# Attention's values in three chunks instead of four, their halves copied by ScalarE and added by GpSimd, one maximum for both context units

## The chip, the cores and the metric

The kernel runs on one core of a Trainium2 chip. The time is the device time of that core in microseconds; the profile is of one execution, taken by the hardware profiler. The engines are TensorE (PE, with its weight loads as PEld), VectorE (DVE), ScalarE (ACT), GpSimd (POOL) and SyncE (SP), which here only starts transfers. They run side by side and each works through its own queue in order.

## The reference

Two layers of a trunk over 1024 latent tokens (8 tiles of 128) and 256 context tokens (2 tiles), width 1024. In each layer a combined projection feeds a convolution, a retention and a latent attention; their outputs are joined, projected and normalised, and a gated feed-forward layer follows. The change touches the attention. It has 8 heads, queries and keys of 96 (64 without position, 32 with), values of 64:

```python
s = jnp.einsum('bqhd,bkhd->bhqk', qi, k).astype(jnp.float32) * scale
p = jax.nn.softmax(s, axis=-1).astype(v.dtype)
return jnp.einsum('bhqk,bkhd->bqhd', p, v)
...
attL = block_attention(qmL, jnp.concatenate([kmC, kmL], axis=1), jnp.concatenate([vmC, vmL], axis=1))
...
attC = block_attention(qmC, kmC, vmC)
```

Latent queries see all 1280 keys; context queries see the 256 context keys, and only in the first of the two layers.

## The kernel before, in words

**Units, batches, heads.** A unit is 128 queries of one head against all keys. Four units are a batch (512 queries), two batches a head, so a layer has 16 batches and 64 units. In layer 0 each head also has two context units (128 queries against 256 keys). One step of the loop at the end of the printed code handles one unit, and the order of the instructions on each engine is the order in which the code is run through (`manual_schedule`).

**A step.** `scores` multiplies queries and keys into a bank S (two such banks; each product is three matmuls, since both operands are split into a high and a low part) and VectorE takes the negative maximum nm. ScalarE writes P = exp(S + nm) and the sums. A step later VectorE transposes P in blocks of 32 x 32 into T (`block_transpose`). When the fourth unit of a batch is transposed, which is in step 0 of the next batch, `blocks` gathers the blocks of T into PT, twelve of sixteen by transfers that SyncE starts and four by GpSimd's copies.

**The values.** `weigh_chunk` multiplies PT with the values vr into a single bank po, in four chunks of 2, 2, 2 and 4 key tiles (`CHUNKS`); even key tiles add up in partitions 0 to 63 of po, odd ones in 64 to 127. The chunks of a batch run one per step from step 1 of the batch after next; the fourth thus falls on step 0 of the one after that. With the last chunk, TensorE spreads the reciprocal sums over a bank mm (L1011; mm is a single buffer too). `normalise` then copies and adds the two halves of po, multiplies by mm's copy on GpSimd and has `store` write the result.

**Context units.** `context_units` runs after the fourth unit of a head's second batch (of the first one in the last head). Both units' scores go into one mm bank, each followed by its own maximum. `direct_transposes` and `direct_weigh` follow one and two steps later and use mm as well.

**Deferred work.** Three lists hold it: `mids` is served between the scores and the exponential of a step, `soon` after the exponential, `steps` at the end of a step; the first argument of `later` is the number of steps. So loads of the next head (`load_head`, `load_v`; tiles kq and vr), the split of its keys and queries into high and low parts (`split_k`, `split_q`: kh and qh by ScalarE, kl and ql by GpSimd) and the stores all have a place by a number. SyncE's queue takes the loads, the gather of PT and the stores in the order in which they are issued.

Of the kernel before, what the change touches and what calls it, by code (L numbers as in the profile page):

```python
# [11 lines left out]
F32 = mybir.dt.float32  # L12
# [4 lines left out]
AX = mybir.AxisListType  # L17
# [26 lines left out]
def body(tc, I, out):  # L44
    nc = tc.nc
    mult, add, sub = ALU.mult, ALU.add, ALU.subtract

    def pool(name, bufs=1, space=None, side=None):
        kw = {}
        if space is not None:  # L50
            kw["space"] = space
        if side is not None:
            kw["side"] = side
        return tc.tile_pool(name=name, bufs=bufs, reuse_waits="tile", **kw)
# [6 lines left out]
    smp = es.enter_context(pool("small", 4))  # L61
# [14 lines left out]
    def bank(tag="mm", cols=512):  # L76
        return pools[tag].tile([128, cols], F32, name=tag, tag=tag)

    def tt(out, a, b, op, eng=None):
        (eng or nc.vector).tensor_tensor(out=out, in0=a, in1=b, op=op)  # L80
# [22 lines left out]
    def mms(ps, xs, start=True, stop=True):  # L103
        for i, (a, b) in enumerate(xs):
            nc.tensor.matmul(ps, lhsT=a, rhs=b, start=start and i == 0, stop=stop and i == len(xs) - 1)  # L105
# [404 lines left out]
    for l in range(L):  # L510
        last = l == L - 1
# [467 lines left out]
        pp_ = ats.enter_context(pool(f"attp{l}", 2, side="right"))  # L979
        tp_ = ats.enter_context(pool(f"attt{l}", 2, side="right"))  # L980
        sm_ = ats.enter_context(pool(f"atts{l}", 1, side="right"))
        CHUNKS = [range(0, 2), range(2, 4), range(4, 6), range(6, 10)]
        E0, E1, E2 = 6, 8, 8

        def scores(u, ps):

            nk = len(u.kts) * 128
            k0 = u.kts[0] * 128
            for c in range(0, nk, 512):
                n = min(512, nk - c)  # L990
                kc = slice(k0 + c, k0 + c + n)
                mms(ps[:, c:c + n], [(u.qh, u.hd.kh[:, kc]), (u.ql, u.hd.kh[:, kc]), (u.qh, u.hd.kl[:, kc])])
            u.nm = smp.tile([128, 1], F32, name="nm", tag="nm")
            nc.vector.reduce_max(out=u.nm, in_=ps[:, :nk], axis=AX.X, negate=True)  # L994
            u.ps = ps[:, :nk]

        def exponentials(u, P):

            nc.scalar.activation(out=P, in_=u.ps, func=AF.Exp, bias=u.nm, accum_out=u.sm)  # L999
            u.P = P  # L1000
# [16 lines left out]
        def blocks(us, T1):  # L1017
            PT = tp_.tile([128, 4, 4, 320], F32, name="PT", tag="PT")
            for s in range(4):
                for a in range(4):  # L1020
                    c = (a + s) % 4
                    o, i = PT[32 * c:32 * c + 32, a], T1[32 * a:32 * a + 32, c]
                    if s:
                        nc.sync.dma_start(out=o, in_=i)
                    else:
                        nc.gpsimd.tensor_copy(o, i)  # L1026
            us[0].PT = PT

        def weigh_chunk(us, i):
# [5 lines left out]
            src = u.PT.rearrange("p a u n -> p (a u) n")  # L1035
            for j in CHUNKS[i]:
                nc.tensor.matmul(u.po[64 * (j % 2):64 * (j % 2) + 64], lhsT=u.hd.v[:, j, :], rhs=src[:, :, j * 32:j * 32 + 32],  # L1037
                                 start=j < 2, stop=j > 7)
            if i < len(CHUNKS) - 1:
                return  # L1040
# [4 lines left out]
        def normalise(us, pr):  # L1045
            u = us[0]
            o = rawp.tile([128, 1024], F32, name="raw", tag="raw")
            o1, o2 = o[:64, :512], o[:64, 512:]
            nc.scalar.copy(o2, u.po[64:128])
            for i in range(2):  # L1050
                nc.scalar.copy(o1[:, 256 * i:256 * i + 256], pr[64 * i:64 * i + 64, :256])
            tt(o2, u.po[0:64], o2, add)
            tt(o1.rearrange("p (u a i) -> p u a i", u=4, a=4), o2.rearrange("p (a u i) -> p u a i", u=4, a=4),
               o1.rearrange("p (u a i) -> p u a i", u=4, a=4), mult, nc.gpsimd)
            steps.later(1, store, u.h, u.g, 0, o1)
# [32 lines left out]
        steps, mids, soon = Ticks(), Ticks(), []  # L1088
# [5 lines left out]
        def after(u, us, T1):  # L1094
# [6 lines left out]
            blocks(us, T1)  # L1101
            for i in range(len(CHUNKS)):
                mids.later(5 + i, weigh_chunk, us, i)
# [7 lines left out]
        def context_units(h):  # L1111
            us = []
            rc = rawp.tile([128, 1024], F32, name="raw", tag="raw")
            ps = bank("mm")
            sums = smp.tile([128, 4], F32, name="sums", tag="sums", bufs=6)
            for a in range(2):
                u = Unit()
                u.h, u.g, u.a, u.hd, u.kts, u.ending = h, 2, a * 128, heads[h], CTX, False
                u.qh, u.ql = (x[:, a * 128:a * 128 + 128] for x in qs[h, 2])
                u.sums, u.sm, u.t = sums, sums[:, a:a + 1], rc[:, 512:]  # L1120
                us.append(u)
                scores(u, ps[:, a * 256:])
            for a, u in enumerate(us):
                exponentials(u, rc[:, a * 256:a * 256 + 256])
            mids.later(2, direct_transposes, us)
            mids.later(3, direct_weigh, us)

        prev = None
        with tc.manual_schedule():
            for ti, (h, g) in enumerate(todo):  # L1130
                if ti == len(todo) - 1:
                    steps.later(E0, load_wo, 0, (0, 1))
                    steps.later(E1, split_wo, 0, (0, 1))
                    steps.later(E2, load_mixed, 0, 0)
                    steps.later(E2, load_mixed, 0, 1)
                    steps.later(E2, load_wo, 0, (2, 3))
                if g == 0:
                    if not last:
                        steps.later(1, split_q, h, 2)
                    if h:  # L1140
                        mids.later(1 if last else 2, load_v, h)
                    else:
                        steps.later(1, split_q, 0, 1)
                    if h < H_MLA - 1:
                        mids.later(1 if last else 2, load_head, h + 1)
                        steps.later(4, split_k, h + 1)
                        steps.later(5, split_q, h + 1, 0)
                        steps.later(7, split_q, h + 1, 1)
                us = []
                direct = ti == len(todo) - 1  # L1150
                T1 = tp_.tile([128, 4, 4, 320], F32, name="T1", tag="T1")
                sums = smp.tile([128, 4], F32, name="sums", tag="sums", bufs=6)
                for a in range(4):
                    u = Unit()
                    u.h, u.g, u.a, u.hd, u.kts, u.ending = h, g, a * 128, heads[h], kvt, ti == len(todo) - 1
                    u.qh, u.ql = (x[:, a * 128:a * 128 + 128] for x in qs[h, g])
                    u.sums, u.sm = sums, sums[:, a:a + 1]
                    us.append(u)
                    if direct:
                        P = T1.rearrange("p c u n -> p (c u n)")[:, a * NTOK:a * NTOK + NTOK]  # L1160
                    else:
                        P = pp_.tile([128, NTOK], F32, name="P", tag="P")
                    scores(u, bank("S", 1536))
                    mids.tick()
                    exponentials(u, P)
                    if prev is not None:
                        after(*prev)
                    late()
                    prev = (u, us, None if direct else T1)
                    if direct:  # L1170
                        u.t = pp_.tile([128, NTOK], F32, name="P", tag="P")
                        mids.later(1 + a, direct_transposes, [u])
                        mids.later(3 + a, direct_weigh, [u])
                    if not last and a == 3 and g == (h < H_MLA - 1):
                        context_units(h)
                    steps.tick()
            while mids.q or steps.q or soon:
                mids.tick()
                late()
                steps.tick()  # L1180
            split_wo(0, (2, 3))
# [60 lines left out]
        for i, t in enumerate(order):  # L1242
            ps = [firsts.pop(t) if i < 2 else project_out(t, 0), project_out(t, 1)]
# [8 lines left out]
            u = (rawp if late else w2).tile([128, 1024], F32, name="raw" if late else "u", tag="raw" if late else "u")  # L1252
# [104 lines left out]
        steps = {}  # L1357
# [33 lines left out]
        for j in range(NJ):  # L1391
            v = steps.pop(j) if j in steps else first_two(j)
            w, x, u, th1 = v.w, feat.op, v.u, v.th
# [133 lines left out]
        while ahead:  # L1527
# [26 lines left out]
            for t in range(4):  # L1554
                ps = bank("po")
# [34 lines left out]
        for t in tiles:  # L1590
# [4 lines left out]
            ps = [bank("mm") for _ in range(2)]  # L1595
# [123 lines left out]
```

## Time and profile before

| | |
|---|---|
| time, median of 3 runs | 3212.92 us (3206.94 to 3214.75) |
| profiled execution, own time | 3220.49 us |
| its span, first to last instruction | 3218.7 us |
| PE busy | 2974.4 us (92%) |
| DVE busy | 2308.2 us (72%) |
| POOL busy | 1490.9 us (46%) |
| ACT busy | 1194.7 us (37%) |
| mean granted TensorE clock | 0.953 |

The attention of layer 0 runs from about 449 to 745 us of the span, that of layer 1 from about 2170 to 2409. The shares of the whole span are averages over stages that are unlike each other, so the prediction reads these two by themselves. A granted clock of 1.00 is 2.4 GHz, 0.50 is 1.2 GHz. Times in a timeline are in us from the start of the span; a bracket at the end of a line is the engine's idle time ahead of it and what ended it.

### The profile page before, as it was taken

The page shows a single profiled execution, that of the slowest core. Times are in us where ns is not written, and L with a number is a line of the kernel's source. Part 1 is how long each engine was busy: PE and PEld are TensorE (multiplying, and loading weights), DVE is VectorE, ACT ScalarE, POOL GpSimd, SP SyncE. Part 2 cuts the span into 40 slices and gives each one's busy share as a digit, 9 for nine tenths or more (in the row PEclk, how much of TensorE's full clock was granted, in tenths as well). Part 3 has the DMA queues.
Part 4 walks back from the last instruction along what each step waited for, and adds up shares of the span by engine and source line. Part 5 has one row for each costly group of instructions (what it writes and reads, how often), then busy time and mean ns, then how long its engine had stood idle before and what let it go on. Part 6 is the DMA issues. An engine that isn't in the chain of part 4 may idle for free. (4 is left out here: it accounts for less than half of the span.)

```text
span 3218.7 us, 39711 instructions
## 1 busy us (share of the span) xinstructions
PE 2974.4 (92%) x13968; PEld 2303.3 (72%) x13968; DVE 2308.2 (72%) x3254; ACT 1194.7 (37%) x2354; POOL 1490.9 (46%) x1187
## 2 busy tenths in 40 slices
PE   7989998889979999999998898989999899999997
PEld 3677875556768888887786676776568678887685
DVE  4387556665887776654888868458966986666998
ACT  4223544444332222224332522445554322223432
POOL 2274535444332333324876355435654433333993
PEclk9999988889989999999999998998999999999998
DMA  7421156656622222223212521146865232223313
GB/s 277 142 64 33 59 177 153 149 143 209 226 89 105 96 92 97 91 82 141 79 59 75 172 69 46 47 154 163 203 174 168 94 132 85 79 79 144 111 65 119
DMA packets 178527, 381.47 MB, mean 119 GB/s; under 512 B 43255, under 2 KB 77687, under 8 KB 178072
## 3 DMA queue, kind: packets, MB, share of 16 engines
q1 hardware_dynamic: 172980, 360.03, 36.3%
q10 hardware_dynamic: 5348, 18.90, 1.4%
q8 instruction: 111, 1.82, 0.2%
q14 instruction: 88, 0.72, 0.1%
HBM read 242.97 MB, written 76.90 MB: 99 GB/s over the span
## 5 line engine op out<-in xcount | busy, mean ns | idle before, releaser
L80 POOL TENSOR_TENSOR wl<-raw,wh 128x512 fp32r<-128x512 f32 (+2 forms) x208 | 388.7, 1881 | 651.6 <-ACT wh L85 641.7
L85 ACT CAST wh<-raw 128x512 fp32r<-128x512 f32 (+2 forms) x305 | 237.5, 796 | 410.0 <-PE pp L105 190.6
L80 DVE TENSOR_TENSOR w<-pp,w 128x512 f32<-128x512 f32 x308 | 207.2, 685 | 188.0 <-PE pp L105 185.8
L994 DVE TENSOR_REDUCE nm<-S 128x1 f32<-128x1280 f32 x128 | 190.0, 1484 | 81.3 <-PE S L105 80.2
L105 PE MATMUL po<-wh,gh 128*128 128x512 f32 x504 | 203.6, 404 | 33.6 <-DVE p L80 26.9
L999 ACT ACTIVATE P<-S,nm 128x1280 f32<-128x1280 f32 x120 | 159.4, 1328 | 198.8 <-DVE nm L994 198.8
L80 POOL TENSOR_TENSOR rr<-rv,mh 128x1 f32<-128x1 f32 (+2 forms) x130 | 93.1, 717 | 280.9 <-DVE rv L190 278.6
L105 PE MATMUL po<-wh,gl 128*128 128x512 f32 x504 | 200.5, 398 | 0.0
L105 PE MATMUL po<-wl,gh 128*128 128x512 f32 x504 | 200.4, 398 | 0.0
L1026 POOL COPY PT<-T 32x1280 f32<-32x1280 f32 x120 | 149.8, 1248 | 109.0 <-DVE T L1091 49.4
L1037 PE MATMUL po<-PT,vr 128*64 128x512 f32 x600 | 167.9, 658 | 27.3 <-issue 22.4
L584 DVE SCALAR_TENSOR_TENSOR cacc<-cy,cw,cacc 128x1295 f32<-128x1295 f32 (+1 forms) x120 | 190.9, 1631 | 0.0
L80 POOL TENSOR_TENSOR gl<-gr,gh 128x512 fp32r<-128x512 f32 x112 | 174.8, 1586 | 25.7 <-ACT gh L85 25.6
L80 POOL TENSOR_TENSOR wl<-sx,wh 128x1024 fp32r<-128x1024 f32 x44 | 109.6, 2490 | 157.4 <-ACT wh L85 157.4
L1091 DVE STREAM_TRANSPOSE T<-P 128x1280 f32<-128x1280 f32 x120 | 180.0, 1500 | 0.0
L105 PE MATMUL S<-kh,qh 96*128 96x512 f32 (+1 forms) x384 | 163.8, 427 | 4.8 <-ACT P L999 2.6
L80 DVE TENSOR_TENSOR raw<-raw 128x512 f32<-128x512 f32 (+1 forms) x96 | 129.5, 1357 | 50.4 <-POOL wl L80 47.2
L80 DVE TENSOR_TENSOR p<-p,po 128x512 f32<-128x512 f32 x224 | 145.1, 675 | 16.4 <-PE po L105 15.9
L105 PE MATMUL S<-kh,ql 96*128 96x512 f32 (+1 forms) x384 | 150.9, 393 | 0.5 <-POOL ql L80 0.2
L105 PE MATMUL S<-kl,qh 96*128 96x512 f32 (+1 forms) x384 | 150.3, 391 | 0.0
L80 DVE TENSOR_TENSOR wl<-raw,wh 128x512 fp32r<-128x512 f32 (+1 forms) x105 | 124.4, 1194 | 27.9 <-ACT wh L85 27.9
L105 PEld LDWEIGHTS po<-wh,gh 128*128 128x128 f32 x504 | 97.4, 193 | 64.3 <-DVE p L80 31.9
(438 smaller groups left out, 8756.8 us busy)
## 6 DMA issues: line engine op xcount, KB each, us to landing
PT<-T SPq DMA_DIRECT2D x360, 160.0 KB
raw<-in_mod_w SPq DMA_DIRECT2D x96, 512.0 KB
raw<-in_ffn_in SPq DMA_DIRECT2D x88, 512.0 KB
gd<-w SPq DMA_DIRECT2D x88, 256.0 KB
gr<-gd SPq DMA_DIRECT2D x32, 512.0 KB
xs<-x ACTq DMA_DIRECT2D x28, 512.0 KB
raw<-in_ffn_out SPq DMA_DIRECT2D x28, 512.0 KB
x<-xs SPq DMA_DIRECT2D x26, 512.0 KB
```

Source lines behind the costliest of these rows:

```text
L80: (eng or nc.vector).tensor_tensor(out=out, in0=a, in1=b, op=op)
L85: nc.scalar.copy(h, t)
L105: nc.tensor.matmul(ps, lhsT=a, rhs=b, start=start and i == 0, stop=stop and i == len(xs) - 1)
L584: nc.vector.scalar_tensor_tensor(out=acc[:, ct, :], in0=y0[:, ct, j:j + AW], scalar=w, in1=acc[:, ct, :], op0=mult, op1=add)
L994: nc.vector.reduce_max(out=u.nm, in_=ps[:, :nk], axis=AX.X, negate=True)
L999: nc.scalar.activation(out=P, in_=u.ps, func=AF.Exp, bias=u.nm, accum_out=u.sm)
L1026: nc.gpsimd.tensor_copy(o, i)
L1037: nc.tensor.matmul(u.po[64 * (j % 2):64 * (j % 2) + 64], lhsT=u.hd.v[:, j, :], rhs=src[:, :, j * 32:j * 32 + 32], start=j < 2, stop=j > 7)
L1091: nc.vector.transpose(out=T1[:, :, u.a // 128].rearrange("p c (k i) -> p k c i", i=32), in_=u.P.rearrange("p (k c i) -> p k c i", c=4, i=32))
```

## The change

- The values of a batch come in three chunks of 2, 4 and 4 key tiles, in steps 1, 2 and 3 of the batch after next. Step 0 is left without one.
- In `normalise` ScalarE copies both halves of po out (the second into a new tile ou), and GpSimd adds them. Before, ScalarE copied one half and VectorE added the other to it.
- `context_units` runs the scores of both units first and takes both maxima with one reduction (nmc).
- In layer 0 `split_k` of the next head and the first `split_q` come one step later.

```diff
-        CHUNKS = [range(0, 2), range(2, 4), range(4, 6), range(6, 10)]
+        CHUNKS = [range(0, 2), range(2, 6), range(6, 10)]
...
-            nc.scalar.copy(o2, u.po[64:128])
+            o3 = sm_.tile([64, 512], F32, name="ou", tag="ou", bufs=2)
+            nc.scalar.copy(o2, u.po[0:64])
+            nc.scalar.copy(o3, u.po[64:128])
             for i in range(2):
                 nc.scalar.copy(o1[:, 256 * i:256 * i + 256], pr[64 * i:64 * i + 64, :256])
-            tt(o2, u.po[0:64], o2, add)
+            tt(o2, o2, o3, add, nc.gpsimd)
...
-                scores(u, ps[:, a * 256:])
+                u.ps = ps[:, a * 256:a * 256 + 256]
+                score_products(u, u.ps)
+            nm = smp.tile([128, 2], F32, name="nmc", tag="nmc")
+            nc.vector.reduce_max(out=nm, in_=ps.rearrange("p (a k) -> p a k", a=2), axis=AX.X, negate=True)
+            for a, u in enumerate(us):
+                u.nm = nm[:, a:a + 1]
...
-                        steps.later(4, split_k, h + 1)
-                        steps.later(5, split_q, h + 1, 0)
+                        steps.later(4 if last else 5, split_k, h + 1)
+                        steps.later(5 if last else 6, split_q, h + 1, 0)
```

`score_products` is the part of `scores` that multiplies; `scores` calls it and then takes the maximum as before.

Three places where the queues of the engines differ. First TensorE in layer 0, at the end of the second batch of a head (mm<-kh,qch are the context scores, mm<-ident,rs the weights). Before:

```order
L1037 MATMUL po<-PT,vr 64x512 x2
L105 MATMUL mm<-kh,qch 128x256
L105 MATMUL mm<-kh,qcl 128x256 [waits Pool_49]
L105 MATMUL mm<-kl,qch 128x256
L105 MATMUL mm<-kh,qch 128x256 [waits DVE_49]
```

And with the change:

```order
L1041 MATMUL po<-PT,vr 64x512 x4
L1015 MATMUL mm<-ident,rs 64x128 [waits DVE_49]
L1015 MATMUL mm<-ident,rs 64x128 x3
L105 MATMUL mm<-kh,qch 128x256 [waits PE_49,Activation_49]
L105 MATMUL mm<-kh,qcl 128x256 [waits Pool_49]
```

The last chunk and the weights have moved ahead of the context scores; the first of these now has a wait for ScalarE, and the second unit's has none for VectorE any more.

Second, ScalarE in layer 0 around the cast of the next head's keys (kh<-kq). Before:

```order
L877 CAST kh<-kq 96x1280 [waits DMAHW5_49,DMAHW4_49]
L999 ACTIVATE P,sums<-S,nm 128x1280 [waits DVE_49,Activation_49]
L1049 COPY raw<-po 64x512 [waits DMAHW2_49,PE_49]
L1051 COPY raw<-mm 64x256 [waits PE_49]
L1051 COPY raw<-mm 64x256
L85 CAST qh<-kq 96x512 [waits DMAHW7_49,DMAHW6_49]
```

With the change:

```order
L1054 COPY raw<-po 64x512 [waits PE_49]
L1055 COPY ou<-po 64x512 [waits Pool_49]
L1057 COPY raw<-mm 64x256 [waits PE_49]
L1057 COPY raw<-mm 64x256
L1003 ACTIVATE P,sums<-S,nm 128x1280 [waits DVE_49,Activation_49]
L877 CAST kh<-kq 96x1280 [waits DMAHW5_49,DMAHW4_49]
```

The copies of po and mm stood behind the cast and one more exponential, and now stand ahead of both.

Third, SyncE in layer 1 at the start of a head (attd_17807 and, with the change, attd_17821 hold the results of a head's first batch, attd_17808 and attd_17822 those of its second). Before:

```order
L1014 DMA attd_17807<-raw 64x512 [waits DMAHW2_49,Pool_49]
L870 DMA vr<-vd_17723 128x10x64 [waits DMAHW3_49,PE_49]
L861 DMA kq<-kd_17818 64x1280 [waits DMAHW4_49]
L862 DMA kq<-krd_16980 32x1280 [waits DMAHW5_49]
L864 DMA kq<-qd_17822 64x1024 [waits DMAHW6_49,Pool_49]
L865 DMA kq<-qrd_17825 32x1024 [waits DMAHW7_49]
L1024 DMA PT<-T_18370 32x1280 [waits DMAHW0_49,DVE_49]
```

With the change:

```order
L1018 DMA attd_17822<-raw 64x512 [waits DMAHW3_49,Pool_49]
L870 DMA vr<-vd_17737 128x10x64 [waits DMAHW4_49,PE_49]
L861 DMA kq<-kd_17832 64x1280 [waits DMAHW5_49]
L862 DMA kq<-krd_16994 32x1280 [waits DMAHW6_49]
L864 DMA kq<-qd_17836 64x1024 [waits DMAHW7_49]
L865 DMA kq<-qrd_17839 32x1024 [waits DMAHW0_49]
L1028 DMA PT<-T_18402 32x1280 [waits DMAHW1_49,DVE_49]
```

The store ahead of the loads was that of a batch finished four steps earlier, and the second batch's store came behind the gather of PT; now the store ahead of the loads is that of the batch finished in the step before.

## Rows read from the trace of the kernel before

**Rows 1.** Page, part 1: busy us, share of the span and instructions of each engine.

```profile
PE 2974.4 (92%) x13968; PEld 2303.3 (72%) x13968; DVE 2308.2 (72%) x3254; ACT 1194.7 (37%) x2354; POOL 1490.9 (46%) x1187
```

**Rows 2.** Stretches, five heads each: us, busy PE, PEld, DVE, ACT, POOL; clock; DMA.

```profile
515.05:707.02 191.97, 166.54 (x732) 99.29 (x734) 129.22 (x120) 91.14 (x160) 92.71 (x70) 0.86 0.59 146
2222.79:2359.09 136.30, 132.22 (x642) 77.64 (x644) 122.90 (x100) 80.74 (x125) 89.68 (x65) 1.00 0.84 199
```

**Rows 3.** List of waits, attention of layer 0, TensorE: us in total, times, longest.

```profile
PE po L1037 <- issue: 20.4, 6, 4.1
PE mm L105 <- DVE nm L994: 15.0, 8, 2.7
```

**Rows 4.** Timeline of layer 0, one wait of the first kind: start, us, engine, line.

```profile
571.78 1.26 ACT L877 CAST kh<-kq 96x1280 fp32r<-96x1280 f32 x1 [3.25 <-DMA kq<-krd]
...
575.00 0.68 DVE L80 TENSOR_TENSOR raw<-po,raw 64x512 f32<-64x512 f32 x1 [3.61 <-ACT raw L1049]
...
575.78 1.12 PE L1037 MATMUL po<-PT,vr 128*64 128x512 f32 x2 [3.08 <-issue]
```

**Rows 5.** Timeline of layer 0, TensorE, two waits of the second kind.

```profile
588.93 0.39 PE L105 MATMUL mm<-kh,qch 96*128 96x256 f32 x1 [1.75 <-DVE nm L994]
...
625.46 0.58 PE L105 MATMUL mm<-kh,qch 96*128 96x256 f32 x1 [1.75 <-DVE nm L994]
```

**Rows 6.** Table by stretches, layer 0; columns as in rows 2, granted clock third last.

```profile
576.00:584.00 8.00, 8.00 (x19) 3.88 (x18) 5.27 (x4) 2.79 (x4) 7.42 (x7) 0.50 0.64 157
626.00:632.00 6.00, 6.00 (x18) 3.56 (x18) 2.72 (x3) 1.73 (x5) 0.00 (x0) 0.50 0.00 0
589.00:609.00 20.00, 19.82 (x106) 12.41 (x107) 15.85 (x15) 9.06 (x18) 6.95 (x6) 1.00 0.64 160
449.28:478.34 29.06, 24.93 (x79) 19.94 (x78) 22.59 (x17) 15.24 (x25) 12.36 (x9) 0.65 0.37 97
```

**Rows 7.** Timeline of layer 1, TensorE at full clock: scores, values, weights.

```profile
2217.31 0.50 PE L105 MATMUL S<-kh,qh 96*128 96x512 f32 x1
...
2219.25 1.08 PE L1037 MATMUL po<-PT,vr 128*64 128x512 f32 x4
2220.26 0.50 PE L105 MATMUL S<-kh,qh 96*128 96x512 f32 x1
...
2236.00 1.94 PE L1037 MATMUL po<-PT,vr 128*64 128x512 f32 x8
2237.77 0.61 PE L1011 MATMUL mm<-ident,rs 128*64 128x128 f32 x8
```

**Rows 8.** Timeline of layer 1: ScalarE's exponentials and copies, VectorE's addition, GpSimd's multiplication.

```profile
2220.94 1.33 ACT L999 ACTIVATE P<-S,nm 128x1280 f32<-128x1280 f32 x1 [1.03 <-DVE nm L994]
...
2224.37 1.33 ACT L999 ACTIVATE P<-S,nm 128x1280 f32<-128x1280 f32 x1 [2.01 <-DVE nm L994]
...
2225.82 0.58 ACT L1049 COPY raw<-po 64x512 f32<-64x512 f32 x1
2226.42 0.75 ACT L1051 COPY raw<-mm 64x256 f32<-64x256 f32 x2
...
2239.76 0.68 DVE L80 TENSOR_TENSOR raw<-po,raw 64x512 f32<-64x512 f32 x1 [0.74 <-ACT raw L1049]
...
2245.58 1.30 POOL L80 TENSOR_TENSOR raw<-raw 64x512 f32<-64x512 f32 x1
```

**Rows 9.** Timelines of layer 1: first load of a head (SyncE), product that needs PT.

```profile
2224.66 0.39 SPq L870 DMA_DIRECT2D vr<-vd  x1
...
2241.24 1.08 PE L1037 MATMUL po<-PT,vr 128*64 128x512 f32 x4 [0.90 <-DMA attd<-raw]
...
2333.64 0.39 SPq L870 DMA_DIRECT2D vr<-vd  x1
...
2350.14 1.08 PE L1037 MATMUL po<-PT,vr 128*64 128x512 f32 x4 [0.83 <-DMA attd<-raw]
```

**Rows 10.** List of waits, layer 0, SyncE's queue: us in total, times, longest.

```profile
SPq L1014 <- POOL raw L80: 21.8, 6, 4.4
```

More of the change, by code (lines that the diff above doesn't have):

```diff
@@ L981, in body, with score_products @@
         sm_ = ats.enter_context(pool(f"atts{l}", 1, side="right"))
-        CHUNKS = [range(0, 2), range(2, 4), range(4, 6), range(6, 10)]
+        CHUNKS = [range(0, 2), range(2, 6), range(6, 10)]
         E0, E1, E2 = 6, 8, 8
         def scores(u, ps):
+            score_products(u, ps)
+            nk = len(u.kts) * 128
+            u.nm = smp.tile([128, 1], F32, name="nm", tag="nm")
+            nc.vector.reduce_max(out=u.nm, in_=ps[:, :nk], axis=AX.X, negate=True)
+            u.ps = ps[:, :nk]
+        def score_products(u, ps):
             nk = len(u.kts) * 128
@@ L992, in scores @@
                 mms(ps[:, c:c + n], [(u.qh, u.hd.kh[:, kc]), (u.ql, u.hd.kh[:, kc]), (u.qh, u.hd.kl[:, kc])])
-            u.nm = smp.tile([128, 1], F32, name="nm", tag="nm")
-            nc.vector.reduce_max(out=u.nm, in_=ps[:, :nk], axis=AX.X, negate=True)
-            u.ps = ps[:, :nk]
         def exponentials(u, P):
```

## The prediction

> **What bounds the kernel now.** Over the whole span TensorE is busy 92% and VectorE 72% [rows 1], but the change touches attention alone, so I read the two stretches of attention by themselves, five heads of each layer in the table by stretches [rows 2]. In layer 0 five heads take 191.97 us, 38.4 us a head, at a mean granted clock of 0.86; in layer 1 they take 136.30 us, 27.3 a head, at 1.00, with TensorE busy for 132.22 us and VectorE for 122.90. So layer 1 is TensorE's work almost without a hole, and layer 0 has holes. The list of waits says which [rows 3]: six at the first value product of a batch, 20.4 us in all, and eight at the scores of the second context unit, 15.0 us.
>
> The first kind is a chain [rows 4]. ScalarE's cast of the next head's keys (kh) stands idle 3.25 us for a load. The exponential and the copies of the batch that has just been weighed queue behind it, VectorE's addition reads the bank of values (po) only at 575.00, and TensorE, which needs that one bank for the next batch, starts at 575.78 after 3.08 us. The second kind is the one maximum between two sets of scores in one bank [rows 5]. After both kinds TensorE's clock falls [rows 6]: eight microseconds at 0.50 (1.2 GHz) behind the first wait, six behind the wait that ended at 625.46, none behind the equal one that ended at 588.93. A mean of 0.86 is 28% of the time at the lower level, 10.7 us a head; with one sure fall and about half a one per head this is some 7 us, or 3.5 us of lost work, for a fall.
>
> I call the four steps of a head's first batch 0 to 3 and those of its second 4 to 7. One step at full clock costs TensorE 1.94 us of scores (2217.31 to 2219.25), 1.01 for two value products (to 2220.26), 1.77 for four (2236.00 to 2237.77) and 0.55 for the weights behind them [rows 7].
>
> **Three chunks, the free step, the earlier end.** A batch's values were 3 × 1.01 + 1.77 = 4.80 us and are 1.01 + 2 × 1.77 = 4.55, so 0.25 is saved in each of 30 batches where TensorE sets the pace: 14 × 0.25 = 3.5 us in layer 0; in layer 1 it is part of the walk below. More important, the last chunk and the copies that free po now come at step 3 or 7 and no more at the next step 0 or 4. ScalarE's copies then stand ahead of the cast of kh, which layer 0 also moves a step back. The 20.4 us go. What is late next is that cast itself: its load lands as before, so the exponential behind it can be late by a microsecond or so, which a slower TensorE covers; I take 1 us in all, 0 to 6.
>
> **One maximum for both context units.** The 15.0 us at the second unit go, with one reduction of 512 columns in place of two of 256; VectorE, with idle time in layer 0, hides it.
>
> **A wait that the edits put in its place in layer 0.** The weights' bank (mm) is one buffer, and the context scores use it too. Before, the weights came a step after the context scores; now they stand right ahead of them, and the scores wait for ScalarE to copy the weights out. With the exponential of step 7 at time 0: its copies start at 1.45, each takes 0.60, and there are now two halves of po ahead of the two of mm (0.37 each) [rows 8], so mm is free at 1.45 + 0.60 + 0.60 + 0.75 = 3.40. TensorE started that step's scores 3.63 us before the exponential (2217.31 and 2220.94) [rows 7, 8] and is done with them, four products and the weights at −3.63 + 1.94 + 1.77 + 0.55 = 0.63. It waits 2.8 us, in heads 1 to 7: 7 × 2.8 = 19.6. Behind it on TensorE's queue stand the scores of the next head, which need nothing from it. By its length this wait lies next to the 3.08 that is followed by the low clock, so I count a fall for each: 7 × 3.5 = 24.5, against some 28 that the clock costs layer 0 now (10.7 / 2 less 1.2 that lies in the waits themselves, six times, and about 3.4 in heads 0 and 7).
>
> Layer 0: −20.4 − 15.0 + 1 + 19.6 − 3.5 + (24.5 − 28) = **−21.8 us**.
>
> **The halves by ScalarE, the sum by GpSimd.** VectorE loses 30 additions of 0.68 us, ScalarE gains 30 copies of 0.58 and GpSimd 30 additions, priced by its multiplication of the same shape at 1.30 [rows 8]. VectorE has 13 us free in the five heads of layer 1 [rows 2], so its 20 us bring nothing by themselves. GpSimd's work in its gaps costs nothing either, except where somebody waits for the store at its end. The Trainium skill (GPSIMD Engine Reference, the opening paragraphs) speaks against such a move: ordinary elementwise arithmetic is roughly twice as fast on the Vector engine. The trace agrees on the ratio, 1.30 to 0.68 [rows 8], but taken as a loss for each batch the rule would add 30 × 0.6 = 18 us, and the rows give it a price only at the store of five batches, inside the next term.
>
> **The store now stands ahead of the loads in layer 1.** This is the term that decides. SyncE's queue starts its transfers in order and waits where one is not ready, as it does for 21.8 us at the stores of layer 0 [rows 10]. In layer 1 a head's loads are issued at step 0 and the gather of the previous batch (PT) behind them. Loads and gather are one unbroken stretch of transfers: from the first load to the first value product that needs the gather it is 2224.66 to 2241.24, 16.6 us, and 2333.64 to 2350.14, 16.5 [rows 9], with TensorE idle 0.90 and 0.83 at the end. Before, the loads waited for the last use of an older head's values at step 0. Now those are free at step 7, but the store of the batch finished at step 7 is in the queue ahead of the loads, and it waits for GpSimd. From the exponential of step 7: copies of po done at 2.65, GpSimd's addition to 3.95, its multiplication to 5.25, the store's issue 0.5, first load at 5.8, gather there at 5.8 + 16.5 = 22.3. TensorE comes to that product sooner than before: 7 × 1.94 of scores, 1.01 + 3 × 1.77 of products, 2 × 0.55 of weights and 0.2 at the free step, where the third scores wait for a bank, 21.2 in all, less 3.63, is 17.6. It waits 4.7 us. A head then takes 22.3 to the product, then 1.01 + 1.94 + 1.77 to the scores of the next step 7 and 3.63 to its exponential: 30.7 against 27.3, +3.4. This holds in the five heads (2 to 6) that have both a store and a full set of loads: +17. Each wait is longer than any that the trace shows in layer 0 ahead of the low clock, so a fall each: 5 × 3.5 = 17.5. The other three heads gain 0.7 each, −2. Layer 0 is spared, since its loads follow the gather.
>
> Layer 1: +17 + 17.5 − 2 = **+32.5 us**.
>
> **Sum.** −21.8 + 32.5 = +10.7 us. The profiled execution took 3220.5 us (span 3218.7), 7.6 above the median of 3212.9 of the three runs shown; the same difference on the median gives **3224 us**, 0.33% slower. Bounds: a fall may cost 2 to 5 us, which over twelve falls moves the sum by −18 to +18, the context wait is 2.2 to 3.1 and the load wait 4.0 to 5.2 (the addition between VectorE's 0.68 and 1.30, the start of the loads 0.5 either way). Together the forecast's own range is 3208 to 3240.
>
> **Rivals.**
> The loads are not held: the store is ready early, or the transfers close up when they start later. For it speaks that the queue would be free and the values are released at step 7; against it the two stretches of equal length and the order of the queue. Layer 1 then gains 0.7 in seven heads, −5, and the total is −27: 3186. Chance 0.17.
>
> The clock holds after the new waits. For it: the 1.75 us wait at 588.93 left it at 1.00; against it: the equal one at 625.46 did not, and both new waits are longer. Without the twelve falls the sum is 10.7 − 24.5 − 17.5 = −31: 3182. Chance 0.10.
>
> Slower by more: behind the context wait come two steps of scores without values, and such a stretch, the start of layer 0 with scores alone, runs at a mean of 0.65 [rows 6]. If the low clock lasts until values are multiplied again, a fall costs 6 us in layer 0 and 4.5 in layer 1: +17.5 + 5, sum +33: 3246. It decides as soon as a fall lasts over 10 us. Chance 0.13.
>
> That VectorE was the limit and its 20 us come back is nearly excluded by its idle time; it would show as a faster layer 1 and has its place in the first rival's chance.
>
> **Chances.** Forecast 0.60, of which 0.34 slower by over 0.3% (about what a measurement of this kernel can tell from no change), 0.21 within, 0.05 faster; the first two rivals 0.27 faster; the third 0.13 slower. Faster 0.32, same 0.21, slower 0.47. The range from 3186 to 3244 leaves out most of the clock rival, some of the first and half of the third.
>
> **What would show it.** In layer 0: no wait of TensorE at the first value product of step 5, none for a maximum, and in heads 1 to 7 one of about 2.8 us at the first context scores, released by ScalarE's copy of mm; 34 to 36 us a head. In layer 1: the store on SyncE ahead of the loads, the first load some 5.8 us behind the exponential of step 7, TensorE idle 4 to 5 us at the values of step 5 and at the lower clock behind it, 33 to 35 us a head. It is wrong if those heads stay at 27, if the stretch from the first load to the product is well under 16.5, or if the clock stays at 1.00 behind waits of this length.

## The result, and the profile after

The changed kernel is **slower by 0.8%**: a median of 3239.97 us in 8 runs (3224.65 to 3242.08) against 3212.14 us for the kernel before in 8 runs beside it, ratio 1.0078, 95% interval [1.0053, 1.0102]. A second comparison gave 3234.98 against 3208.94 us, ratio 1.0076 [1.0058, 1.0093]. The prediction named 3224 us, slower, in a range of 3186 to 3244.

The profile of the changed kernel is of an execution of 3225.29 us (span 3223.3, mean clock 0.956). A second one, of 3235.91 us (span 3233.9, clock 0.954), stands nearer to the median, so I read both. The page's part 1 (columns as in [rows 1]) of the first:

```profile
PE 2956.5 (92%) x13968; PEld 2294.7 (71%) x13968; DVE 2286.3 (71%) x3216; ACT 1208.8 (38%) x2384; POOL 1527.7 (47%) x1217
```

VectorE lost 22 us and GpSimd gained 37: the addition moved as told. The time is decided elsewhere. The stretches of heads 2 to 6 in both layers, as in [rows 2], of the first profile and then of the second:

```profile
512.56:675.08 162.52, 147.29 (x731) 94.33 (x731) 120.78 (x106) 96.00 (x170) 105.82 (x80) 0.95 0.73 173
2188.82:2359.48 170.66, 142.28 (x641) 83.83 (x640) 115.71 (x91) 85.06 (x135) 101.83 (x76) 0.88 0.69 159
```

```profile
510.09:679.89 169.80, 154.90 (x731) 100.52 (x731) 120.97 (x105) 96.36 (x170) 105.59 (x80) 0.90 0.70 165
2189.36:2365.39 176.03, 145.81 (x641) 85.15 (x640) 115.69 (x90) 85.00 (x135) 101.65 (x76) 0.85 0.67 154
```

In layer 0 five heads fell from 191.97 us to 162.52 and 169.80; in layer 1 they grew from 136.30 to 170.66 and 176.03. Layer 1 was at a clock of 1.00 [rows 2] and is now at 0.88 and 0.85.

**What PE waits for now.** From the list of waits of the first profile, layer 0 and then layer 1 (columns as in [rows 3]):

```profile
PE mm L105 <- ACT raw L1057: 18.4, 7, 2.6
```

```profile
PE po L1041 <- DMA attd<-raw: 16.5, 3, 6.2
PE po L1041 <- DMA PT<-T: 10.1, 2, 5.1
```

Both kinds of [rows 3] are gone. In layer 0 seven waits for the bank mm have taken their place, and layer 1 has five at the values of step 5, put down to the store three times and to the gather twice; both are on one queue.

**The wait in layer 0**, in the timeline of the second profile (a head's step 7), and the same instruction in the first:

```profile
535.92 1.33 ACT L1003 ACTIVATE P<-S,nm 128x1280 f32<-128x1280 f32 x1 [1.33 <-DVE nm L990]
...
537.24 0.57 ACT L1054 COPY raw<-po 64x512 f32<-64x512 f32 x1
537.83 0.58 ACT L1055 COPY ou<-po 64x512 f32<-64x512 f32 x1
538.43 0.74 ACT L1057 COPY raw<-mm 64x256 f32<-64x256 f32 x2
...
539.23 0.58 PE L105 MATMUL mm<-kh,qch 96*128 96x256 f32 x1 [2.63 <-ACT raw L1057]
```

```profile
541.14 0.39 PE L105 MATMUL mm<-kh,qch 96*128 96x256 f32 x1 [2.63 <-ACT raw L1057]
```

The copies are those of the forecast, one behind the other: PE starts 3.31 us behind the exponential (the bank was forecast free at 3.40) and has waited 2.63 us (2.8 forecast). The length of the first product tells the clock: 0.58 us in the one profile, 0.39 in the other. The table by stretches of the two, just behind these waits, confirms it (granted clock third last):

```profile
539.20:546.00 6.80, 6.77 (x20) 5.72 (x21) 2.58 (x3) 1.32 (x5) 2.32 (x2) 0.50 0.09 19
```

```profile
541.10:547.10 6.00, 5.96 (x33) 4.50 (x34) 3.90 (x5) 2.64 (x7) 2.56 (x3) 1.00 0.10 22
```

Behind waits of the same length PE runs at 1.2 GHz for 6.8 us in one execution and at 2.4 GHz in the other. In the first profile five of the seven waits are followed by the lower clock, in the second all seven, and heads 2 to 6 take 7.3 us longer there. The other three heads of layer 0 take 3.5 us less, so 3.8 of the 10.6 us between the two spans are in layer 0; 5.1 are in layer 1.

**The wait in layer 1**, in the timeline of the first profile, from the exponential of a head's step 7 on:

```profile
2185.69 1.33 ACT L1003 ACTIVATE P<-S,nm 128x1280 f32<-128x1280 f32 x1 [1.51 <-DVE nm L990]
...
2188.25 1.29 POOL L80 TENSOR_TENSOR raw<-raw,ou 64x512 f32<-64x512 f32 x1
2189.61 1.28 POOL L80 TENSOR_TENSOR raw<-raw 64x512 f32<-64x512 f32 x1
...
2190.92 0.48 SPq L1018 DMA_DIRECT2D attd<-raw  x1
2191.50 0.53 SPq L870 DMA_DIRECT2D vr<-vd  x1
...
2209.36 1.98 PE L1041 MATMUL po<-PT,vr 128*64 128x512 f32 x4 [5.66 <-DMA attd<-raw]
```

The store goes out when GpSimd is done, and the first load stands behind it, 5.81 us after the exponential (5.8 forecast). From there to the product it is 17.86 us, where [rows 9] had 16.6 and 16.5. In the five heads of each of the two profiles the load starts 5.8 us behind the exponential, and the stretch from it to the product is 16.4 to 17.9 us, once 19.9.

### The profile page after: what moved, and what is told of

It is laid out like the page before. It is cut to its first block, busy times and chain, and to the rows that moved or that the text cites. A ratio compares the mean times of both kernels' runs of the same rounds, so it can differ in the third digit from the quotient of the medians.

```text
span 3223.3 us, 39755 instructions
## 1 busy us (share of the span) xinstructions
PE 2956.5 (92%) x13968; PEld 2294.7 (71%) x13968; DVE 2286.3 (71%) x3216; ACT 1208.8 (38%) x2384; POOL 1527.7 (47%) x1217
## 5 line engine op out<-in xcount | busy, mean ns | idle before, releaser
L105 PE MATMUL po<-wh,gh 128*128 128x512 f32 x504 | 204.0, 405 | 34.2 <-DVE p L80 27.3
L1041 PE MATMUL po<-PT,vr 128*64 128x512 f32 x600 | 157.5, 640 | 27.7 <-DMA attd<-raw 16.5
```

## The experiments

E0, the second profile above, was the changed kernel itself:

> The changed kernel itself, beside the others on one chip: ratio to before 1.008 again. Its profile serves to see where the usual execution, some 15 us longer than the profiled one, spends its time. Theory: it has more stretches of low clock behind the same waits (mean clock 0.951 to 0.954 against 0.956), and no further wait. Rival: waits that are longer, of transfers above all, at an equal clock.

Measured: 3234.98 us, ratio 1.0076. The first theory holds: the waits in layer 0 are the same, 18.4 us in seven, and the mean clock is lower. The rival has a part: the waits at step 5 in layer 1 are 28.5 us in place of 26.6, one of them 8.2 us.

**E1: the loads ahead of the store.**

```diff
-            steps.later(1, store, u.h, u.g, 0, o1)
+            steps.later(2 if last else 1, store, u.h, u.g, 0, o1)
```

> The changed kernel, with the store of a batch one step later in layer 1 alone, so that the next head's loads stand ahead of it on SyncE's queue. Theory (the loads are held by a store that waits for GpSimd): the first load goes out at the free step itself, 4 to 6 us earlier, TensorE's five waits of 4.7 to 6.2 us at the values of step 5 shrink to under 1 us, the low clock behind them goes, and heads 2 to 6 of layer 1 come back from 34.1 us to 27 each: some 32 us less than the changed kernel, a ratio to the kernel before of about 0.998. Rival (the transfers or the free step are what is slow, whatever stands ahead of them): the waits at step 5 and 33 to 34 us a head stay, ratio 1.007. Layer 0 is unchanged in both.

Measured: 3193.24 us, ratio 0.9943 [0.9926, 0.9960], 42 us less than the changed kernel beside it. Heads 2 to 6 of layer 1 in the table by stretches, then the first load and the product of step 5 in the timeline:

```profile
2188.42:2323.26 134.84, 129.58 (x641) 77.83 (x640) 114.63 (x91) 85.48 (x136) 102.36 (x76) 1.00 0.83 201
```

```profile
2185.32 1.33 ACT L1003 ACTIVATE P<-S,nm 128x1280 f32<-128x1280 f32 x1 [1.52 <-DVE nm L990]
...
2185.86 0.54 SPq L870 DMA_DIRECT2D vr<-vd  x1
...
2203.21 1.08 PE L1041 MATMUL po<-PT,vr 128*64 128x512 f32 x4
```

The first load starts 0.54 us behind the exponential in place of 5.81 (0.9 to 1.6 in the four other heads), the product has no wait (no bracket; its data were there when PE came, 17.35 us behind the load; 0.6 us at most in the other heads), and a head takes 27.0 us at a clock of 1.00. Layer 1 is 212.7 us long, 2.1 less than before. So the store that waits for GpSimd, ahead of the loads, is shown to be the cause of what these heads lost.

**E2: the context scores ahead of the weights.**

```diff
-                    if not last and a == 3 and g == (h < H_MLA - 1):
+                    if not last and a == 2 and g == (h < H_MLA - 1):
```

> The changed kernel, with the two context units of a head begun one step earlier, so that their scores stand ahead of the batch's weights in the order for the single bank mm. Theory (the bank is what the context scores wait for): the seven waits of 2.6 us go, 18 us, and with them a few stretches of low clock of 3.5 us of lost work: 18 to 35 us less than the changed kernel, ratio to before 0.997 to 1.002. Rival (the wait only moves: the weights now wait for the exponentials of the context units, which read the same bank): a wait of 2 to 3 us at the weights or behind them in each of seven heads, and no change, ratio 1.007. Layer 1 is unchanged in both.

Measured: 3203.07 us, ratio 0.9980 [0.9966, 0.9993], 32 us less than the changed kernel. Heads 2 to 6 of layer 0:

```profile
502.89:649.71 146.82, 142.98 (x730) 88.38 (x730) 120.47 (x106) 95.75 (x171) 106.12 (x81) 1.00 0.81 191
```

The 2.63 us waits are gone, the clock is 1.00 throughout, and a head takes 29.4 in place of 34.0 us. Of the rival 2.3 us are left: the transposes of the context units (L1070) now wait for the copy of mm, seven times, 0.7 us at most. Span less PE's busy time is 3.84 us for five heads where the second profile had 14.90, so 2.2 of the 4.6 us a head are idle time and 2.4 are the clock. The wait for the single bank is the cause.

**E3: both edits, of E1 and E2.**

> Both edits at once: the store of layer 1 one step later, the context units of layer 0 one step earlier. If the two terms stand alone, each gives what it gave by itself, 32 and 18 to 35 us, in all 50 to 67 less than the changed kernel: ratio to before 0.987 to 0.993. If layer 1's clock or transfers depend on what layer 0 leaves behind, or both edits feed one cause, the sum is smaller than the parts.

Measured: 3166.79 us, ratio 0.9864 [0.9846, 0.9882], 68 us less than the changed kernel, where the parts gave 42 and 32, 74 in all. The five heads of layer 0 and of layer 1 show that the two terms stand alone; they take what they took in E2 and in E1:

```profile
504.57:651.40 146.83, 143.03 (x730) 88.38 (x730) 120.46 (x105) 95.61 (x171) 106.09 (x81) 1.00 0.81 191
2162.62:2297.46 134.84, 129.52 (x641) 77.85 (x640) 114.64 (x91) 85.45 (x136) 102.33 (x76) 1.00 0.83 200
```

So the four edits are worth 1.4% once the two orders that they upset are mended.

**E4: the old end of a batch.** In the changed kernel, VectorE adds again:

```diff
-            nc.scalar.copy(o2, u.po[0:64])
-            nc.scalar.copy(o3, u.po[64:128])
+            nc.scalar.copy(o2, u.po[64:128])
...
-            tt(o2, o2, o3, add, nc.gpsimd)
+            tt(o2, u.po[0:64], o2, add)
```

> The changed kernel with the old end of a batch: one ScalarE copy of po, and VectorE adds the halves. Theory (the addition matters only where someone waits for the store or for the weights' bank): the store is ready 0.6 to 1.3 us earlier, so TensorE's five waits in layer 1 shorten from 5 to about 4 us, the seven context waits from 2.6 to 2.0, the low clock behind them stays, and the sum is 10 us less than the changed kernel, ratio to before about 1.0045. Rival (VectorE is what limits, and its additions cost what they last): 30 times 0.68, 20 us more than the changed kernel, ratio 1.014. Second rival (GpSimd's addition costs a batch 0.6 us each): 18 us less, ratio 1.002.

Measured: 3212.32 us, ratio 1.0015 [1.0005, 1.0026], some 20 us less than the changed kernel's ratio, twice what I expected. From the list of waits and the table by stretches, layer 0:

```profile
PE mm L105 <- ACT raw L1055: 15.2, 7, 2.2
```

```profile
506.72:664.10 157.38, 144.79 (x731) 92.31 (x730) 127.09 (x115) 90.99 (x161) 93.01 (x70) 0.97 0.75 178
```

The waits shortened as told (2.17 us here, 3.8 to 4.6 in layer 1). What I missed is the clock: only two of the seven waits of 2.17 us are followed by the lower level, and layer 0 stands at 0.97. The size is that of the second rival, 0.6 us a batch, but the place is not: it lies at the two kinds of wait, as E9 shows.

**E9: the same edit where no wait is left**, on E3.

> The changed kernel with both orders mended (store of layer 1 a step later, context units a step earlier) and the old end of a batch: one ScalarE copy, VectorE adds. Theory (the place of the addition has a price only through a wait that it lengthens, and here no such wait is left): within 5 us of the kernel with both orders mended and GpSimd's addition, ratio 0.985 to 0.988. Rival (VectorE's 30 additions of 0.68 us come back as time): 10 to 20 us slower than that, ratio 0.990 to 0.993. Rival (GpSimd's addition costs 0.6 us a batch wherever it stands): 18 us faster than that, ratio 0.981.

Measured: 3170.59 us, ratio 0.9870 [0.9845, 0.9895], against 0.9864 for E3: no difference that the intervals show. The five heads of each layer, against 146.83 and 134.84 us in E3:

```profile
504.32:651.13 146.81, 142.58 (x732) 88.41 (x731) 126.99 (x115) 91.02 (x160) 93.39 (x71) 1.00 0.80 191
2159.89:2293.52 133.63, 128.13 (x641) 77.92 (x640) 121.03 (x101) 80.80 (x126) 89.43 (x65) 1.00 0.85 204
```

VectorE is busy some 6.5 us longer in each stretch, and neither stretch is longer. Where nobody waits for it the place of the addition is free here, and VectorE's 20 us do not come back as time.

**E5, E6, E7: single edits on the kernel before**: the one maximum, the later keys and queries, the three chunks.

```diff
-                scores(u, ps[:, a * 256:])
+                u.ps = ps[:, a * 256:a * 256 + 256]
+                score_products(u, u.ps)
+            nm = smp.tile([128, 2], F32, name="nmc", tag="nmc")
+            nc.vector.reduce_max(out=nm, in_=ps.rearrange("p (a k) -> p a k", a=2), axis=AX.X, negate=True)
```

```diff
-                        steps.later(4, split_k, h + 1)
-                        steps.later(5, split_q, h + 1, 0)
+                        steps.later(4 if last else 5, split_k, h + 1)
+                        steps.later(5 if last else 6, split_q, h + 1, 0)
```

```diff
-        CHUNKS = [range(0, 2), range(2, 4), range(4, 6), range(6, 10)]
+        CHUNKS = [range(0, 2), range(2, 6), range(6, 10)]
```

> The kernel before with the one maximum for both context units and nothing else. Theory: the eight waits for the maximum, 15.0 us, go, and with them the low clock behind about half of them, 10 to 14 us: 15 to 29 us less than before, ratio 0.991 to 0.995. Rival (the exponentials behind it start later, because the single reduction of 512 columns ends after both sets of scores): the wait moves to whoever needs the weights of the context units, and the ratio is 0.998 to 1.000.

> The kernel before with only the preparation of the next head's keys and queries one step later in layer 0. Theory (the six long waits at the first value product come from the copies that queue on ScalarE behind the idle cast of kh): the copies now stand ahead of the cast, the waits of 20.4 us go, with them six stretches of low clock of some 3.5 us lost: 20 to 40 us less than before, ratio 0.9875 to 0.994. Rival (the bank po is late for another reason: four chunks keep it busy into the next batch): the waits stay, ratio 1.000; or the cast, now later, holds up the next head, ratio over 1.000.

> The kernel before with only the three chunks of values in place of four, so with the free step, but with the addition on VectorE, the keys at their old step and the maximum for each context unit. Theory (the chunks alone bring both new waits): no long wait at the first value product in layer 0, but the eight waits for the maximum stay or grow, seven waits of about 2.0 us for the weights' bank join them, and in layer 1 five waits of 4 us for transfers that stand behind the store: a ratio to before of 1.005 to 1.012, slower than the changed kernel or equal to it. Rival (the chunks by themselves are a gain and the other edits spoil it): 0.25 us a batch and the 20 us of waits, ratio 0.990 to 0.994.

Measured: E5 3190.41 us, ratio 0.9945 [0.9927, 0.9963]; E6 3176.93 us, 0.9908 [0.9892, 0.9924]; E7 3253.07 us, 1.0143 [1.0125, 1.0160]. From the lists of waits of layer 0, E5, E6 and E7 in this order:

```profile
PE po L1041 <- issue: 23.1, 6, 4.6
```

```profile
PE mm L105 <- DVE nm L994: 16.1, 8, 3.9
```

```profile
PE S L105 <- ACT P L999: 21.3, 9, 4.0
PE mm L105 <- ACT raw L1051: 13.0, 6, 2.2
PE mm L105 <- DVE nm L994: 6.5, 7, 3.4
```

E5 loses the second kind and keeps the first; E6 the other way round. In E6's timeline the copy of po, with four chunks as before, stands ahead of the cast:

```profile
558.88 0.58 ACT L1049 COPY raw<-po 64x512 f32<-64x512 f32 x1
...
560.14 1.26 ACT L877 CAST kh<-kq 96x1280 fp32r<-96x1280 f32 x1
```

So moving the keys by a step is enough for the long waits; the chunks aren't needed for it. E7's timeline shows the other half:

```profile
529.89 1.26 ACT L877 CAST kh<-kq 96x1280 fp32r<-96x1280 f32 x1 [2.46 <-DMA kq<-krd]
531.17 1.33 ACT L999 ACTIVATE P<-S,nm 128x1280 f32<-128x1280 f32 x1
...
532.64 0.50 PE L105 MATMUL S<-kh,qh 96*128 96x512 f32 x1 [2.63 <-ACT P L999]
```

The chunks alone take the copies from behind the cast, but an exponential stays behind it, and 21 us appear as waits for the score banks that it has to read. Layer 0's attention is as long as before (289.6 us, 290.6 before), and layer 1 has the store in its way (five heads 164.49 us). E7 came out slower than I expected, for the first reason.

**E8: the two edits that gain, without the two others**: the diffs of E5 and E6 together.

> The kernel before with two parts of the change, the one maximum and the keys a step later in layer 0, and without the other two: four chunks and VectorE's addition stay. Theory (a head of layer 0 has its low clock as long as one of the two kinds of waits is left, so that the parts give more together than one by one, 19 and 33 us): both kinds of waits are gone, the clock of layer 0 stays at 1.00 from the second head on, a head takes 28.5 to 29.5 us there and 27.2 in layer 1, and the kernel is 50 to 65 us faster than before, ratio 0.980 to 0.985. Rival (the parts only add up, or one takes the other's gain): ratio 0.984 to 0.990, with a wait left in each head.

Measured: 3165.31 us, ratio 0.9863 [0.9838, 0.9887]. Layer 0, table and list of waits:

```profile
502.57:655.37 152.80, 144.95 (x732) 88.38 (x734) 128.09 (x115) 91.13 (x160) 92.98 (x70) 1.00 0.75 183
```

```profile
PE S L105 <- POOL ql L80: 9.9, 7, 2.7
```

The clock holds, but in each head 1.2 us are left for the low half of the queries (ql), which GpSimd now makes a step later. The product of the single ratios is 0.9853, so the rival was right in the sum: the parts add up. The theory has a part in it: layer 0 of the profiled executions has 85 us at the lower clock in the kernel before, 61 in E5, 51 in E6 and 7 in E8, more together than one by one, and the new waits, 9.9 us, take that back. Two of the four edits give what all four give with both orders mended.

**E10: E8 with GpSimd's addition**: the new end of a batch, as in the diff of the change.

> The kernel before with the one maximum, the keys a step later, and the new end of a batch: two halves of po copied by ScalarE and added by GpSimd; four chunks stay. Theory (no one waits for the end of a batch here, since the values of the next batch come long after po is free and the loads go ahead of the store): within 5 us of the same kernel with VectorE's addition. Rival (VectorE, with 123 of 136 us busy in layer 1, was a brake): 5 to 15 us faster than that. Rival (ScalarE's further copy delays the exponentials behind it): 5 to 18 us slower.

Measured: 3191.85 us, ratio 0.9944 [0.9929, 0.9960], 26 us slower than E8; my theory fell. The list of waits of layer 0, and GpSimd's queue ahead of one of them:

```profile
PE S L105 <- POOL ql L80: 18.4, 7, 2.8
```

```profile
497.51 1.29 POOL L80 TENSOR_TENSOR raw<-raw,ou 64x512 f32<-64x512 f32 x1
498.88 1.27 POOL L80 TENSOR_TENSOR raw<-raw 64x512 f32<-64x512 f32 x1
500.12 2.91 POOL L80 TENSOR_TENSOR kl<-kq,kh 96x1280 fp32r<-96x1280 f32 x1
502.98 2.50 POOL L80 TENSOR_TENSOR ql<-kq,qh 96x512 fp32r<-96x512 f32 x2
```

The added 1.3 us stand ahead of kl and ql, PE waits 2.76 us for them in place of 1.2 in six heads, and the clock of the five heads of layer 0 falls to 0.94. In layer 1 ql is waited for too, 6.7 us in place of 0.5, and five heads take 141.90 us in place of 136.56. That ScalarE's copy delays the exponentials does not show: PE's waits for them in layer 0 are 3.3 us against 4.2 in E8. Neither rival named the place; the store wasn't the only one waiting behind GpSimd.

**E11: E8 with ql made by VectorE in layer 0.**

```diff
-                        steps.later(5 if last else 6, split_q, h + 1, 0)
+                        steps.later(5 if last else 6, split_q, h + 1, 0, None if last else nc.vector)
```

> The kernel before with the one maximum and the keys and queries a step later in layer 0, and the low half of the queries (ql) subtracted by VectorE in place of GpSimd in layer 0. In the run without this last edit TensorE waits 1.2 us in six heads for ql, which stands on GpSimd's queue behind the end of the batch and kl. Theory (GpSimd's order is what the scores of the next head wait for): the six waits go, heads 2 to 6 take 29.4 in place of 30.6 us, 7 to 8 us less, ratio 0.983 to 0.985. Rival (the wait passes to VectorE, or to the cast of qh ahead of it): 30 to 31 us a head, ratio 0.986 or more.

Measured: 3161.94 us, ratio 0.9852 [0.9824, 0.9880]. Heads 2 to 5 take 29.8 us in place of 30.6, without the wait, but in head 6 of the profiled run PE waited 3.5 us anew, and that head took 34.4. The medians differ by 3.4 us, and the interval takes in that of E8: whether it is faster stays open. E3, E8, E9 and E11 all beat both kernels, by 1.3 to 1.5% against the kernel before, and can't be told apart.

## Why the prediction was right, and where it was off

The sign, the mechanism and the places were right; the time was 16 us low, at the upper end of the forecast's own range (3240). By layer, from the first to the last maximum of its scores, against the kernel before (290.6 and 214.8 us):

| us | forecast | first profile | second profile |
|---|---|---|---|
| layer 0 | -21.8 | -32.2 | -28.4 |
| layer 1 | +32.5 | +34.5 | +39.6 |
| rest of the span | 0 | +2.3 | +4.0 |
| sum | +10.7 | +4.6 | +15.2 |

The sum came out nearer than its parts: in the second profile layer 0 is 6.6 us below its forecast and layer 1 7.1 above, and that the two nearly cancel is luck.

- **The long waits, -20.4**: gone. The step named two causes at once, the earlier end and the later cast. E6 shows that the later cast does it alone, E7 that the earlier end alone moves the loss to the score banks.
- **The maximum, -15.0**: gone. E5 gives 18 us (0.55%) for it; the long waits were left, and the clock of the five heads rose only from 0.86 to 0.88.
- **The wait for mm, +19.6**: 18.4, in the seven heads named. E2 gives 32 us for it and its falls.
- **The falls in layer 0, 24.5 - 28**: all seven came in the second profile, with 6.7 to 6.8 us at the lower clock behind five of them and 3.4 behind two, so 3.4 and 1.7 of lost work, 3.5 forecast. The first profile had five, two of them of 3.4 us, hence 31 to 34 us a head there. On the other side of the difference I was short: the second profile has 42.5 us at the lower clock in heads 1 to 7, the kernel before 64.9 by the same count, so 11 us came back where I reckoned 3.5.
- **Chunks, -0.25 a batch**: not seen by itself. In layer 1 E3 takes 27.0 us a head, E9 26.7 and E8, with four chunks, 27.3: 0.3 to 0.6 against the 0.5 a head reckoned. These kernels differ in the order of the stores too.
- **The store ahead of the loads, +32.5**: E1 gives 42 us for it. The start, 5.8 us, held in all ten heads of the two profiles; the waits were 4.7 to 6.2 us and once 8.2 in place of 4.7, since the stretch from load to product was 16.4 to 17.9 us and once 19.9 in place of 16.5. Behind the waits the lower clock lasted 3.3 to 9.3 us, so 1.6 to 4.6 of lost work: 15.2 us for the five in the first profile and 19.0 in the second, where 17.5 was forecast.
- **GpSimd's addition, nothing by itself**: right where nobody waits (E9), wrong as a general statement, since its queue holds more than the store (E10). On the rule of the Trainium skill (GPSIMD Engine Reference, the opening paragraphs) the trace keeps its ratio, 1.29 to 0.68 us. Its 18 us as a loss of each batch is nearly what E4 measured, by accident: the loss sits in twelve waits and is not seen in E9.
- **The rest of the span, put at nothing**: behind the last maximum of layer 1 the eight profiles with three chunks take 838.5 to 842.4 us and the six with four 833.8 to 836.9, some 4.5 us more on the mean. The forecast had no term for it, and its cause stays open.
- **The step that fell short is the last one of the sum.** I carried the difference from the profiled execution of before to the median and got 3224. That execution was at 3220.5 us and a clock of 0.953; the 17 of the kernel before beside E0 lie at 3200.3 to 3218.6 with clocks of 0.956 to 0.967, so it stands 11.5 us above their median, where the second profile of the changed kernel (3235.91 us) stands 0.9 above its own. The difference of the medians is 26 to 28 us in place of 10.7: beside E0 some 11 of the missing 15 are the base, 4.5 the sum (15.2 in the second profile). Where in the kernel these 11 us lay stays open. The 27.3 us of low clock in the first two heads of layer 1 do not tell it: the same code had 27.3 there in E5, 23.9 in E11, 13.7 in E8 and 6.8 in E6, and the two heads took 52.9 us in the kernel before and in E5 and 49.8 in E6, 3 us less.

Of the rivals, that the loads are not held fell with E1. That the clock holds was true in layer 0 for two waits of the first profile and for none of the second; in layer 1 the lower clock stood behind all ten. The median, 3239.97 us, lies nearer to the third rival's 3246 than to 3224, but the rival's mechanism does not make up the difference: its larger term was in layer 0, and there no fall behind a wait lasted longer than 6.8 us. In layer 1, where it put a fall at 4.5 us of lost work, the mean is 3.0 and 3.8 in the two profiles.

## To carry to other kernels

Read a queue as the thing that is moved: an edit that finishes a batch a step earlier changes which instruction stands ahead of which on SyncE, GpSimd and a single bank, and here two such orders cost 68 us (E3) while the edits themselves were worth 42. Undo the orders before undoing the edits, and try the edits one by one: two of the four gave all the gain. And where executions of one kernel differ, look how far the profiled one lies from its median before you carry its difference over: here that step lost more than any term of the sum.

## What the runs showed of the hardware

- **The length of a wait does not decide whether the clock falls.** 1.2 us: none of six (E8). 1.75 us: all seven in E6, three of six in the kernel before. 2.17 us: two of seven (E4). 2.63 us: five of seven in one execution of the changed kernel, seven of seven in the next. 2.76 us: five of six (E10). What else decides stays open.
- **VectorE and GpSimd get in each other's way when VectorE reads two tiles beside GpSimd's work.** E11's timeline, VectorE's subtraction that makes ql and GpSimd's instructions beside it, in two heads:

```profile
521.00 2.57 POOL L1030 COPY PT<-T 32x1280 f32<-32x1280 f32 x2
523.20 0.91 DVE L80 TENSOR_TENSOR ql<-kq,qh 96x512 fp32r<-96x512 f32 x1 [0.63 <-ACT qh L85]
523.64 1.61 POOL L80 TENSOR_TENSOR raw<-raw 64x512 f32<-64x512 f32 x1
...
642.97 1.27 POOL L80 TENSOR_TENSOR raw<-raw 64x512 f32<-64x512 f32 x1
643.70 3.98 DVE L80 TENSOR_TENSOR ql<-kq,qh 96x512 fp32r<-96x512 f32 x1 [1.79 <-ACT qh L85]
644.21 2.92 POOL L80 TENSOR_TENSOR kl<-kq,kh 96x1280 fp32r<-96x1280 f32 x1
```

With GpSimd idle, at 436.28 us of the same span, the subtraction takes 0.69 us. In the first of these heads it begins in the last 0.37 us of GpSimd's copies (to 523.57) and takes 0.91, and GpSimd's multiplication, begun meanwhile, takes 1.61 in place of 1.27; heads 1 to 5 are all like this. In the second it begins during GpSimd's multiplication, GpSimd's kl follows at once, and it takes 3.98, to 647.68, where kl ends at 647.13. The maximum behind it on VectorE is late, and so are the exponential and PE: that is the 3.5 us that E11 lost in one head. The Trainium skill (SBUF — State Buffer, SBUF: two separate sides) says that a VectorE instruction with two inputs in SBUF and a GpSimd instruction that reads SBUF share a pair of ports, which whoever starts first holds for a whole instruction, while the other is blocked. These lines agree with it: the subtraction ends 0.54 and 0.55 us behind the end of GpSimd's instructions.
